# Half of the weights' remainders formed by accumulating DMAs instead of VectorE

## The chip, the cores and the metric

The kernel runs on one core of a Trainium2 chip. The metric is the time of one execution in microseconds on the device; times named here are the median of several runs, and a profile is one further execution, with its own time. The engines are called by their names in the profile: PE (TensorE, the matmuls), DVE (VectorE), ACT (ScalarE), POOL (GpSimd) and SP (SyncE, which here only issues DMAs).

## The reference

The reference is a trunk of two layers on x of 512 tokens by 1024 channels, in float32. Cut to what matters:

```python
for i in range(DEPTH):                       # DEPTH = 2
    xn = rmsnorm(x, norm1_g[i])
    u_pool, q, k, v, g_a, g_b = split(xn @ w_in[i])     # one combined projection
    q = partial_rotary(rmsnorm(q, q_norm_g[i])); k = partial_rotary(rmsnorm(k, k_norm_g[i]))
    o = diff_attention(q, k, v, lam)         # 4 heads, each two softmaxes of 128-wide q and k:
                                             # (p0 - lam * p1) @ v, chunk-causal with chunks of 64
    attn_out = rmsnorm(o, subln_g[i]) * (1.0 - lam_init)
    pool_out = pool_mixer(u_pool, pool_w[i], pool_scale[i])   # windowed means, 4 groups
    merged = sigmoid(g_a) * pool_out + sigmoid(g_b) * attn_out
    x = x + merged @ w_out[i]
    gate, up = split(rmsnorm(x, norm2_g[i]) @ w_ffn_in[i])
    x = x + (silu(gate) * up) @ w_ffn_out[i]
return x
```

## The kernel before

Every product is made in three matmuls of a reduced float format (fp32r): an operand is split into a rounded part, called hi, and its remainder, lo, and a product is hi·hi + hi·lo + lo·hi. So each weight has to be split before PE can use it. The weights come in pieces of 128 x 1024 numbers (512 KB): SP issues a load into a tile `raw` (line 213; seven slots), ACT casts it to `whi`, and DVE subtracts, `wlo = raw - whi` (both line 201, in `split`; six slots each). For some pieces of the feed-forward part there is already another way, lines 225 to 227 in `parts`: ACT casts to `whi`, ACT writes the negated piece, rounded, to `wlo`, and POOL issues a DMA that loads the same piece from memory a second time and adds it to `wlo`. The result is again weight minus rounded weight.

PE's work is written out in program order by the functions below, with a clock of PE columns: `later(delay, what)` queues a step until that clock has gone on by `delay`, and `run_due` starts due steps between matmuls. The order on each engine follows from that and from the scheduler that takes an instruction as its inputs come ready.

In each layer the heads are taken in the order 3, 2, 1, 0 (`ORDER`). A head has three blocks of weights, each of four pieces (`wblock(KD)`, 1024 by 512): the first for q and k, the second for v and one gate (both in `attention`), the third for the pooled branch and the other gate (in `merged`, run behind the next head's attention; the last one behind its own). For each quarter of the tokens (t = 0 to 3) `evicted` makes the squares of q and k (ACT, line 585), a power on POOL (line 335, `r`), and the scaled copy `qn` on DVE (line 589). Outside the first head of layer 0 the transpose goes partly through memory: DVE transposes into `near` (line 305), SP writes it to `away` and reads it back to `near` (lines 306 and 310), and ACT and DVE split it into `qh` and `ql`. Then `scores` multiplies q and k into one of two banks `sc`, ACT takes the exponential (`pr`, line 520), `turn_prob` splits the probabilities into `ah` and `al`, and `weighted` multiplies them with v. The same detour by `near` serves the probabilities and the head's output (`mt`).

The first block of layer 0's head 3 is read by another path (`at_start`) and doesn't come by `wblock`.

Of the kernel before, what the change touches and what calls it, by code (L numbers as in the profile page):

```python
# [23 lines left out]
KD = D // P  # L24
# [26 lines left out]
ORDER = (3, 2, 1, 0)  # L51
# [72 lines left out]
def trunk_kernel(  # L124
# [16 lines left out]
    def mm_ps():  # L141
        return ps.tile([P, 512], F32, name="mm", tag="mm", bufs=6)
# [60 lines left out]
    def split_half(hi, lo, src):  # L203

        half = nc.scalar.activation(hi, src, AF.Copy, scale=0.5)
        return half, nc.vector.scalar_tensor_tensor(lo, src, 0.5, hi.bitcast(F32), op0=ALU.mult, op1=ALU.subtract)

    def loaded():

        i = at[0]  # L210
        at[0] += 1
        raw = sb.tile([P, 2, 512], F32, name="raw", tag="raw", bufs=RAWS)
        transfers.append(nc.sync.dma_start(raw.rearrange("p a b -> p (a b)"), wts[i]))
        return raw, i
# [3 lines left out]
    def parts(raw, piece_no=None):  # L218

        hi = sb.tile([P, 2, 512], F32R, name="whi", tag="whi", bufs=SPLITS)  # L220
        lo = sb.tile([P, 2, 512], F32R, name="wlo", tag="wlo", bufs=SPLITS)
        if piece_no is None:
            made[:] = split(hi, lo, raw)
        else:
            nc.scalar.copy(hi, raw)
            made[0] = nc.scalar.activation(lo, raw, AF.Copy, scale=-1.0)  # L226
            nc.gpsimd.dma_start(lo.rearrange("p a b -> p (a b)"), wts[piece_no], accum_op=ALU.add)  # L227
        return hi, lo

    def rows_of(pair, n=2):  # L230

        hi, lo = (x.rearrange("p a b -> p (a b)").rearrange("p (k c) -> p k c", k=n) for x in pair)
        return [(hi[:, k, :], lo[:, k, :]) for k in range(n)]

    def piece(n=2, by_dma=False):
        raw, i = loaded()
        return rows_of(parts(raw, i if by_dma else None), n)

    def wblock(n):

        return [pair for _ in range(n // 2) for pair in piece()]


    clock = [0]
# [40 lines left out]
    def product(acc, pairs):  # L285

        n = len(pairs)
        for i, ((ah, al), (bh, bl)) in enumerate(pairs):
            run_due()
            nc.tensor.matmul(acc, lhsT=ah, rhs=bh, start=i == 0, stop=False)  # L290
            nc.tensor.matmul(acc, lhsT=ah, rhs=bl, start=False, stop=False)  # L291
            last = nc.tensor.matmul(acc, lhsT=al, rhs=bh, start=False, stop=i == n - 1)  # L292
            clock[0] += 3 * acc.shape[-1]
        return last
# [48 lines left out]
    def need(*keys):  # L343
        run_due(lambda: all(k in ready for k in keys))
# [9 lines left out]
    def pair(name, tag, n):  # L354
        return [sb.tile([P, n, S], F32R, name=name + part, tag=tag, bufs=2) for part in "hl"]
# [117 lines left out]
    for layer in range(L):  # L473
# [8 lines left out]
        def x_all(t0=0, t1=NT):  # L482
            return [(xh[:, k, t0 * P:t1 * P], xl[:, k, t0 * P:t1 * P]) for k in range(KD)]

        def cut(pairs, c0, c1):
            return [(h[:, c0:c1], l[:, c0:c1]) for h, l in pairs]

        def attention(j, before, then):

            if before is not None:  # L490
# [84 lines left out]

            at_start = not layer and j == ORDER[0]
            if not at_start:
                w = wblock(KD)
            held = []

            def evicted(t, acc):
# [33 lines left out]
                need(*((layer, before, "o", t) for t in range(NT)))  # L615
            vh, vl = pair("v", "v", 2)
            tb = [sb.tile([P, 2, VD], F32, name="tb", tag="tb", bufs=2) for _ in range(2)]
            w = wblock(KD)
            if at_start:
                with tc.issue_after(transfers[-1].ins):  # L620
                    for i in range(L):
# [14 lines left out]
        def pool_weights(j):  # L636
            raw = sb.tile([P, 2, VD], F32, name="pwr", tag="raw", bufs=RAWS)
            nc.scalar.dma_start(raw.rearrange("p a b -> p (a b)"), pool_w[layer, j])
            both = sb.tile([P, 2, 2, VD], F32R, name="pw", tag="pw")
            hi, lo = both[:, 0], both[:, 1]  # L640
            split(hi, lo, raw)
            return [(hi[:, a, :], lo[:, a, :]) for a in range(2)]

        def windowed(j, c, acc, uh, ul):

            window = WINDOWS[j]
            up = sb.tile([P, 16 + S], F32, name="up", tag="up", bufs=2)
            nc.vector.memset(up[:, :16], 0.0)
            nc.vector.tensor_mul(up[:, 16:], acc, rms_rows[layer])
            prev, step, n = up, 1, 0  # L650
            while step < window:
                cur = sb.tile([P, 16 + S], F32, name="us", tag="us", bufs=2)
                nc.vector.memset(cur[:, :16], 0.0)
                nc.vector.tensor_add(cur[:, 16:], prev[:, 16:], prev[:, 16 - step:16 + S - step])
                prev, step, n = cur, step * 2, n + 1
            head = sb.tile([P, 16], F32, name="head", tag="head", bufs=2)
            nc.vector.tensor_mul(head, prev[:, 16:32], inv_t[:, j, :])
            nc.vector.scalar_tensor_tensor(
                prev[:, 32:], prev[:, 32:], 1.0 / window, up[:, 32:], op0=ALU.mult, op1=ALU.subtract)
            nc.vector.tensor_sub(prev[:, 16:32], head, up[:, 16:32])  # L660
            split(uh[:, c, :], ul[:, c, :], prev[:, 16:])

        def merged(j, mj, mh, ml):

            w = wblock(KD)
            pw = pool_weights(j)
            uh, ul = pair("u", "u", 2)
            for c in range(2):
                acc = mm_ps()
                product(acc, list(zip(cut(w, c * P, (c + 1) * P), x_all())))  # L670
                windowed(j, c, acc, uh, ul)

            gates = []
            for c in range(2):
                acc = mm_ps()
                product(acc, list(zip(cut(w, VD + c * P, VD + (c + 1) * P), x_all())))
                ta = sb.tile([P, S], F32, name="ta", tag="ta", bufs=2)
                nc.vector.tensor_mul(ta, acc, rms_rows[layer])
                nc.scalar.activation(ta, ta, AF.Tanh, scale=0.5)
                gates.append(ta)  # L680
            need(*((layer, j, "mj", t) for t in range(NT)))
            for c in range(2):
                y = mm_ps()
                product(y, list(zip(cut(pw, c * P, (c + 1) * P), [(uh[:, a, :], ul[:, a, :]) for a in range(2)])))
                ta = gates[c]
                k = KD * layer + 2 * j + c
                nc.vector.scalar_tensor_tensor(ta, ta, 1.0, y, op0=ALU.add, op1=ALU.mult)
                nc.vector.scalar_tensor_tensor(ta, ta, scale[:, k:k + 1], mj[:, c, :], op0=ALU.mult, op1=ALU.add)
                split_half(mh[:, c, :], ml[:, c, :], ta)
# [257 lines left out]
        def mix(i):  # L947
            j = ORDER[i]
            if i == 2:
                need(*((layer, ORDER[3], "s", t) for t in range(NT)))  # L950
                ms[j] = pair("m", "qk", 4)
            else:
                ms[j] = pair("m", "m", 2)
            merged(j, mjs[j], *ms[j])

        for i, j in enumerate(ORDER):
            then = (lambda: project_out(ORDER[i - 2])) if i >= 2 else None
            mjs[j] = attention(j, ORDER[i - 1] if i else None, then)
            if i:
                mix(i - 1)  # L960
# [68 lines left out]
```

## Time and profile before

| | |
|---|---|
| median of 3 runs | 1392.16 us (1390.02 to 1392.28) |
| the profiled execution | 1391.49 us, span of its instructions 1389.7 us |
| mean granted clock of PE | 0.997 |
| PE busy | 1375.8 us, 99% of the span |
| DVE / ACT / POOL busy | 1042.5 / 704.1 / 118.2 us |
| pieces of weights split by DVE | 221 subtractions, 266.7 us |
| pieces with an accumulating DMA | 64, all in the feed-forward parts |
| moved by DMA | 224.52 MB |

In the rows of the profile an operation stands with its line, the engine and "output <- inputs"; x is the count, then come the busy time and the mean of one in nanoseconds, and behind a bar the idle time of the engine just before and what ended it. A row of the timeline has the start, the duration, the engine and the line, and in brackets the idle time before it with its releaser. A row of waits has the waiting operation, the one waited for, the total in microseconds, the count and the longest. A row of stretches has the stretch, the busy time of PE, PE's weight loads, DVE, ACT and POOL with counts, the granted clock, the share of the DMA engines and GB/s. A row of a DMA queue has packets, megabytes and the share of sixteen engines' span.

### The profile page before, as it was taken

What the parts mean: (1) busy time and instruction counts of PE and PEld (TensorE: products, weight loads), DVE (VectorE), ACT (ScalarE), POOL (GpSimd) and SP (SyncE); (2) the same over time, 40 slices, a digit from 0 to 9 for tenths busy, and PEclk for the clock granted to TensorE, in tenths of its full rate; (3) what the DMA queues carried; (4) which work ended last, traced back from release to release, by engine and by line L of the source; (5) the groups of instructions that cost most, each with busy time, mean ns of one, the idle gap of its engine ahead of it and who ended that gap; (6) DMA issues with size and microseconds to landing.
All of it is one profiled execution on the core that took longest, in us unless ns stands there. A gap on an engine that the chain in (4) does not pass through costs nothing.

```text
span 1389.7 us, 18568 instructions
## 1 busy us (share of the span) xinstructions
PE 1375.8 (99%) x6242; PEld 1142.0 (82%) x6242; DVE 1042.5 (75%) x1979; ACT 704.1 (51%) x1321; POOL 118.2 (9%) x139
## 2 busy tenths in 40 slices
PE   9999999999999999999999889999999999999999
PEld 7888888888888888888888778888888888888887
DVE  7778778786869768578667787786868686785782
ACT  7545353454766545564435443444547565554540
POOL 1010100000111001110011100000001010011100
PEclk9999999999999999999999999999999999999999
DMA  8333454444667868686334345534446688687741
GB/s 311 104 124 112 147 162 131 148 136 134 152 181 191 240 177 225 164 208 209 109 121 137 106 135 165 163 122 148 140 129 151 183 199 220 195 219 173 199 129 61
DMA packets 141071, 224.52 MB, mean 162 GB/s; under 512 B 40880, under 2 KB 88496, under 8 KB 140976
## 3 DMA queue, kind: packets, MB, share of 16 engines
q1 hardware_dynamic: 130464, 187.65, 42.1%
q0 software_dynamic: 9216, 33.56, 13.8%
q10 hardware_dynamic: 1296, 2.12, 0.5%
q8 instruction: 49, 0.80, 0.2%
q14 instruction: 46, 0.38, 0.1%
HBM read 194.04 MB, written 29.23 MB: 161 GB/s over the span
## 4 chain that ended last, share of the span: by engine, by line
PE 93%; DVE 3%; issue 1%; DMA 1%; POOL 1%; ACT 0%; SPq 0%; DVEq 0%; POOLq 0%; ACTq 0%
PE mm L272 14%; PE mm L273 14%; PE mm L271 14%; PE mm L292 13%; PE mm L290 13%; PE mm L291 13%; PE sc L271 3%; PE sc L273 3%; PE sc L272 3%; PE sc L291 1%; PE sc L292 1%; PE sc L290 1%; DVE qn L589 1%; POOL r L335 1%; DVE wlo L201 1%
## 5 line engine op out<-in xcount | busy, mean ns | idle before, releaser
L201 DVE TENSOR_TENSOR wlo<-raw,whi 128x1024 fp32r<-128x1024 f32 (+1 forms) x221 | 266.7, 1211 | 62.9 <-ACT whi L201 62.3
L201 ACT CAST whi<-raw 128x1024 fp32r<-128x1024 f32 (+1 forms) x221 | 229.9, 1047 | 165.0 <-PE mm L273 60.3
L290 PE MATMUL mm<-whi,xh 128*128 128x512 f32 x480 | 189.0, 394 | 0.0
L291 PE MATMUL mm<-wlo,xh 128*128 128x512 f32 x480 | 187.5, 391 | 0.0
L292 PE MATMUL mm<-whi,xl 128*128 128x512 f32 x480 | 187.3, 390 | 0.0
L273 PE MATMUL mm<-fh,wlo 128*128 128x512 f32 (+1 forms) x356 | 137.8, 387 | 0.0
L272 PE MATMUL mm<-fl,whi 128*128 128x512 f32 (+1 forms) x356 | 137.8, 387 | 0.0
L271 PE MATMUL mm<-fh,whi 128*128 128x512 f32 (+1 forms) x356 | 137.8, 387 | 0.0
L692 DVE TENSOR_TENSOR res<-mm,res 128x512 f32<-128x512 f32 (+1 forms) x145 | 98.1, 680 | 43.1 <-PE mm L273 41.8
L292 PEld LDWEIGHTS mm<-whi,xl 128*128 128x128 f32 x480 | 90.3, 188 | 19.2
L290 PEld LDWEIGHTS mm<-whi,xh 128*128 128x128 f32 x480 | 90.4, 188 | 17.4
L291 PEld LDWEIGHTS mm<-wlo,xh 128*128 128x128 f32 x480 | 90.5, 188 | 17.2
L227 POOL DMA_DIRECT2D wlo<-in_wts x64 | 56.1, 877 | 536.8 <-ACT wlo L226 364.1
L335 POOL TENSOR_TENSOR r<-r,mhalf 128x1 f32<-128x1 f32 (+1 forms) x64 | 56.4, 882 | 528.8 <-DVE r L334 509.0
L291 PE MATMUL mm<-xl,whi 128*128 128x512 f32 x256 | 100.4, 392 | 0.0
L290 PE MATMUL mm<-xh,whi 128*128 128x512 f32 x256 | 100.3, 392 | 0.0
L292 PE MATMUL mm<-xh,wlo 128*128 128x512 f32 x256 | 100.0, 391 | 0.0
L273 PE MATMUL mm<-whi,xl 128*128 128x512 f32 x224 | 87.2, 389 | 0.0
L271 PE MATMUL mm<-whi,xh 128*128 128x512 f32 x224 | 87.2, 389 | 0.0
L272 PE MATMUL mm<-wlo,xh 128*128 128x512 f32 x224 | 87.2, 389 | 0.0
L226 ACT ACTIVATE wlo<-raw 128x1024 fp32r<-128x1024 f32 x64 | 67.7, 1057 | 29.0 <-PE mm L272 27.3
L271 PEld LDWEIGHTS mm<-fh,whi 128*128 128x128 f32 x356 | 66.9, 188 | 13.6
(217 smaller groups left out, 2939.4 us busy)
## 6 DMA issues: line engine op xcount, KB each, us to landing
raw<-in_wts SPq DMA_DIRECT2D x243, 512.0 KB, 3.9
wlo<-in_wts POOLq DMA_DIRECT2D x64, 512.0 KB, 6.1
away<-near SPq DMA_DIRECT2D x72, 256.0 KB, 2.4
near<-away SPq DMA_DIRECT2D x288, 64.0 KB, 2.5
away<-near SPq DMA_DIRECT2D x28, 128.0 KB, 1.7
near<-away SPq DMA_DIRECT2D x112, 32.0 KB, 2.5
pwr<-in_pool_w ACTq DMA_DIRECT2D x8, 256.0 KB, 2.7
away<-pr SPq DMA_DIRECT2D x7, 256.0 KB, 2.0
```

Of the source, the lines that this page charges most:

```text
L201: return nc.scalar.copy(hi, src), nc.vector.tensor_sub(lo, src, hi.bitcast(F32))
L226: made[0] = nc.scalar.activation(lo, raw, AF.Copy, scale=-1.0)
L227: nc.gpsimd.dma_start(lo.rearrange("p a b -> p (a b)"), wts[piece_no], accum_op=ALU.add)
L271: nc.tensor.matmul(acc, lhsT=ah, rhs=bh, start=start, stop=False, **check)
L272: nc.tensor.matmul(acc, lhsT=ah, rhs=bl, start=False, stop=False, **check)
L273: last = nc.tensor.matmul(acc, lhsT=al, rhs=bh, start=False, stop=stop, **check)
L290: nc.tensor.matmul(acc, lhsT=ah, rhs=bh, start=i == 0, stop=False)
L291: nc.tensor.matmul(acc, lhsT=ah, rhs=bl, start=False, stop=False)
L292: last = nc.tensor.matmul(acc, lhsT=al, rhs=bh, start=False, stop=i == n - 1)
L335: nc.gpsimd.tensor_tensor(r, r, mhalf[:, :width], op=ALU.pow)
L589: nc.vector.scalar_tensor_tensor(qn[:, h, :], acc[:, h * QK:(h + 1) * QK], r[:, h:h + 1], g, op0=ALU.mult, op1=ALU.mult)
L692: return nc.vector.tensor_add(res[d][:, cs], acc, res[d][:, cs])
```

## The change

In every block of every head, except the blocks of head 3 in layer 0, the first two of the four pieces now get their remainder in the way of lines 225 to 227: a cast and a negated copy on ACT, and an accumulating DMA issued by POOL. The other two pieces stay with DVE. That is 9 blocks in layer 0 and 12 in layer 1, so 42 pieces. Lines behind the new function carry numbers three higher than before.

```diff
-    def wblock(n):
-
-        return [pair for _ in range(n // 2) for pair in piece()]
+    def wblock(n, by_dma=0):
+
+        return [pair for i in range(n // 2) for pair in piece(2, i < by_dma)]
...
+        def by_dma(j):
+            return 2 if layer or j != ORDER[0] else 0
+
         def attention(j, before, then):
...
             if not at_start:
-                w = wblock(KD)
+                w = wblock(KD, by_dma(j))
...
-            w = wblock(KD)
+            w = wblock(KD, by_dma(j))
             if at_start:
...
         def merged(j, mj, mh, ml):
 
-            w = wblock(KD)
+            w = wblock(KD, by_dma(j))
             pw = pool_weights(j)
```

The scheduler puts the instructions in another order in places. On DVE, in the first head of layer 1 (at 717 to 723 us of the profile before; `wlo_7050` and `wlo_7056` are remainders of the block for v, `near_6714` the transposed q and k of a quarter), the row before was:

```order
L201 TENSOR_TENSOR wlo_6799<-raw_6796,whi_6798 128x1024
L362 TENSOR_TENSOR m12_6709<-qn_6695,tab_68 128x128
L366 TENSOR_TENSOR m12_6709<-qn_6695,tab_68 128x4x16 x2
L201 TENSOR_TENSOR wlo_7050<-raw_7047,whi_7049 128x1024
L367 TENSOR_TENSOR qn_6695<-m12_6709 128x4x32
L201 TENSOR_TENSOR ql_6527<-near_6635,qh_6526 128x4x128
L201 TENSOR_TENSOR wlo_7056<-raw_7053,whi_7055 128x1024
L305 STREAM_TRANSPOSE near_6714<-qn_6695 128x4x4x32
```

and now, at the same place on DVE (other numbers for the same tiles), it is:

```order
L201 TENSOR_TENSOR wlo_6821<-raw_6818,whi_6820 128x1024
L362 TENSOR_TENSOR m12_6729<-qn_6715,tab_68 128x128
L366 TENSOR_TENSOR m12_6729<-qn_6715,tab_68 128x4x16 x2
L201 TENSOR_TENSOR ql_6545<-near_6655,qh_6544 128x4x128
L367 TENSOR_TENSOR qn_6715<-m12_6729 128x4x32
L305 STREAM_TRANSPOSE near_6734<-qn_6715 128x4x4x32
```

Two subtractions are gone, and ql stands one place further ahead.

On PE, at 57 to 61 us, in layer 0, the scores of the first head's last quarter (`sc_633` and `sc_640`) stood in the middle of the second head's projection (`mm_679`):

```order
L290 MATMUL mm_679<-whi_663,xh_113 128x512
L291 MATMUL mm_679<-wlo_664,xh_113 128x512
L292 MATMUL mm_679<-whi_663,xl_114 128x512
L290 MATMUL mm_679<-whi_663,xh_113 128x512
L291 MATMUL mm_679<-wlo_664,xh_113 128x512
L290 MATMUL sc_633<-qh_230 128x512
L291 MATMUL sc_633<-ql_231,qh_230 128x512
```

and now stand on PE three matmuls earlier in it (`mm_681` is that projection's tile in the changed program):

```order
L290 MATMUL mm_681<-whi_664,xh_113 128x512
L291 MATMUL mm_681<-wlo_665,xh_113 128x512
L290 MATMUL sc_633<-qh_230 128x512
L291 MATMUL sc_633<-ql_231,qh_230 128x512
L292 MATMUL sc_633<-qh_230,ql_231 128x512
L290 MATMUL sc_640<-qh_230 128x512
L291 MATMUL sc_640<-ql_231,qh_230 128x512
L292 MATMUL sc_640<-qh_230,ql_231 128x512
L292 MATMUL mm_681<-whi_664,xl_114 128x512
```

Three matmuls of the projection moved behind the six of the scores. The same happens at 744 us, in layer 1, with two matmuls; the rest of PE's order is as before.

On POOL the issues now stand between the powers of line 335. Its order in layer 0, from 30 us on (`r_357` is the power of the first head's last quarter), was:

```order
L335 TENSOR_TENSOR r_326<-r_326,mhalf_69 128x4
L335 TENSOR_TENSOR r_357<-r_357,mhalf_69 128x4
L335 TENSOR_TENSOR r_705<-r_705,mhalf_69 128x1
L335 TENSOR_TENSOR r_722<-r_722,mhalf_69 128x4
L335 TENSOR_TENSOR r_790<-r_790,mhalf_69 128x1
```

and is now, on POOL:

```order
L335 TENSOR_TENSOR r_326<-r_326,mhalf_69 128x4
L227 DMA wlo_658<-in_wts 128x1024
L335 TENSOR_TENSOR r_357<-r_357,mhalf_69 128x4
L227 DMA wlo_665<-in_wts 128x1024
L227 DMA wlo_1002<-in_wts 128x1024
L227 DMA wlo_1009<-in_wts 128x1024
L335 TENSOR_TENSOR r_707<-r_707,mhalf_69 128x1
```

One issue came ahead of the fourth power, and three came between it and the fifth. Each waits for the negated copy on ACT that precedes it.

## The prediction

> **What bounds the kernel now.** I read the page first, for the engines' shares, the chain that ended last and the price of each operation.
>
> ```profile
> PE 1375.8 (99%) x6242; PEld 1142.0 (82%) x6242; DVE 1042.5 (75%) x1979; ACT 704.1 (51%) x1321; POOL 118.2 (9%) x139
> ...
> q0 software_dynamic: 9216, 33.56, 13.8%
> ...
> PE 93%; DVE 3%; issue 1%; DMA 1%; POOL 1%; ACT 0%; SPq 0%; DVEq 0%; POOLq 0%; ACTq 0%
> ...
> L201 DVE TENSOR_TENSOR wlo<-raw,whi 128x1024 fp32r<-128x1024 f32 (+1 forms) x221 | 266.7, 1211 | 62.9 <-ACT whi L201 62.3
> ...
> L227 POOL DMA_DIRECT2D wlo<-in_wts x64 | 56.1, 877 | 536.8 <-ACT wlo L226 364.1
> ...
> L226 ACT ACTIVATE wlo<-raw 128x1024 fp32r<-128x1024 f32 x64 | 67.7, 1057 | 29.0 <-PE mm L272 27.3
> ...
> wlo<-in_wts POOLq DMA_DIRECT2D x64, 512.0 KB, 6.1
> ```
>
> PE is busy 99% of the span and makes 93% of the chain. VectorE, which the change relieves, has 3% of the chain. So relief pays only where PE stands still. Busy time in stretches shows where that is, and PE's waits show on whom:
>
> ```profile
> 100.00:700.00 600.00, 599.97 (x2707) 499.34 (x2706) 460.26 (x808) 312.60 (x537) 46.57 (x53) 1.00 0.59 165
> 700.00:750.00 50.00, 49.14 (x231) 40.92 (x230) 35.16 (x99) 23.03 (x68) 5.84 (x6) 1.00 0.41 133
> 750.00:800.00 50.00, 46.16 (x215) 38.20 (x214) 37.25 (x103) 23.89 (x71) 6.45 (x8) 0.97 0.39 116
> 800.00:850.00 50.00, 46.40 (x209) 38.01 (x208) 39.05 (x99) 17.75 (x52) 5.01 (x6) 0.97 0.50 157
> ```
>
> ```profile
> PE mm L290 <- ACT ah L201: 6.4, 2, 3.2
> ...
> PE sc L290 <- ACT pr L520: 0.9, 1, 0.9
> PE sc L291 <- DVE ql L201: 0.5, 1, 0.5
> PE mm L292 <- DVE up L648: 0.4, 1, 0.4
> ```
>
> From 100 to 700 us, which holds most of layer 0's changed heads, PE idles 0.03 us in 600. The idle time to be had is at the start of layer 1: 0.86, 3.84 and 3.60 us. The waits end on ACT's casts of the probabilities (ah, twice, 3.2 us the longest), on an exponential (pr), and on DVE's ql and up. None ends on a wlo, the tile the change makes in another way.
>
> **The change, part by part.** It removes 42 subtractions on DVE: 42 x 1.211 = 51 us. It adds 42 negated copies on ACT (42 x 1.057 = 44 us) and 42 DMA issues on POOL (42 x 0.877 = 37 us), each of 512 KB that lands after 6.1 us. The 64 such DMAs of before take 13.8% of sixteen engines' span, 191.8 us, or 3.0 us each; 42 more take 126 us. All these engines have room on average (ACT 51%, POOL 9%), and none of the totals is on PE's path. The first two pieces of a block fill the two spare slots of the six-slot ring, so their remainders are made about a block ahead of use; the 0.9 + 6.1 us of issue and landing is covered by that lead, and if it were gone PE would wait up to those 7 us per block. The raw tile is now freed by ACT's negated copy instead of DVE's subtraction; the loads queued on SP behind it have seven slots of lead. So the sum is made stall by stall.
>
> *Stall A, 3.24 us at 769.6.* PE waits for ah:
>
> ```profile
> 769.60 0.39 PE L290 MATMUL mm<-vh,ah 128*128 128x256 f32 x1 [3.24 <-ACT ah L201]
> ```
>
> ```profile
> 765.73 0.39 ACT L555 ACTIVATE mt<-mm 128x256 f32<-128x256 f32 x1 [2.05 <-DVE near L305]
> ...
> 766.10 2.92 ACT L201 CAST whi<-raw 128x1024 fp32r<-128x1024 f32 x3
> 768.93 0.62 ACT L201 CAST ah<-pr 128x512 fp32r<-128x512 f32 x1
> ```
>
> ```profile
> 765.26 0.43 DVE L305 STREAM_TRANSPOSE near<-mt 128x256 f32<-128x256 f32 x1
> ...
> 766.42 1.22 DVE L201 TENSOR_TENSOR wlo<-raw,whi 128x1024 fp32r<-128x1024 f32 x1
> ```
>
> Three whi casts of 2.92 us stand ahead of ah on ACT, and they start when DVE's near (765.26) lets the square at 765.73 go. DVE's work behind that is the eviction of a projection that PE triggers at 753; the timeline has no subtraction on DVE there until 766.42, after the trigger. In the changed order the three casts still stand ahead of ah, and both negated copies behind it. Change 0; between 0 and +1.06, one negated copy, if ACT came to it sooner.
>
> *Stall B, 3.15 and 0.40 us at 817 to 821.* Its chain runs through DVE's work on the pooled branch:
>
> ```profile
> 820.61 0.39 PE L290 MATMUL mm<-vh,ah 128*128 128x256 f32 x1 [3.15 <-ACT ah L201]
> ```
>
> ```profile
> 803.69 0.69 DVE L649 TENSOR_TENSOR up<-mm,hg 128x512 f32<-128x512 f32 x1 [1.86 <-PE mm L292]
> ```
>
> DVE idles 1.86 us before 803.69 for PE, so what it saves on the two subtractions ahead of that becomes longer idling, and no subtraction follows until 826. Change 0.
>
> *Stall C, 0.86 us at 732.4*, is the one with removed work on its chain:
>
> ```profile
> 719.25 1.22 DVE L201 TENSOR_TENSOR wlo<-raw,whi 128x1024 fp32r<-128x1024 f32 x1
> ...
> 720.58 0.69 DVE L201 TENSOR_TENSOR ql<-near,qh 128x512 fp32r<-128x512 f32 x1
> 721.18 1.22 DVE L201 TENSOR_TENSOR wlo<-raw,whi 128x1024 fp32r<-128x1024 f32 x1
> 722.32 0.71 DVE L305 STREAM_TRANSPOSE near<-qn 128x512 f32<-128x512 f32 x1
> ```
>
> ```profile
> 729.96 0.61 ACT L201 CAST qh<-near 128x512 fp32r<-128x512 f32 x1
> 730.59 1.28 ACT L520 ACT_TABLE_LOAD   x1
> 731.88 0.37 ACT L520 ACTIVATE pr<-sc,mx 128x128 f32<-128x128 f32 x1
> ```
>
> ```profile
> 732.39 0.39 PE L290 MATMUL sc<-qh 128*128 128x256 f32 x1 [0.86 <-ACT pr L520]
> ```
>
> ```profile
> 720.00:730.00 10.00, 10.00 (x52) 8.45 (x51) 7.76 (x22) 3.27 (x14) 1.01 (x1) 1.00 0.71 233
> ```
>
> Both subtractions go, so near starts not at 722.32 but where the rest of DVE's row allows, at about 720.2: 2.1 us earlier. But near then goes out to memory and comes back by DMA before qh (end of near 723.03 to qh 729.96, 6.9 us), and the two remainders of this block now travel at that very time: their negated copies end at about 718 and 720.5, and with the landing of 6.1 us they are under way to 727. They ask 2 x 3.0 = 6.0 us of all DMA engines in a window that is 0.71 full and has 2.9 of 10 us free. The round trip grows by between 0 and 6.0 us; I take 2.1, a little under the overflow of 3.1, since part of the first DMA is over before near goes out. Then gain and loss cancel: stall C changes by 0, between -0.86 and +3.9 (6.0 less 2.1).
>
> *Two places where PE's own order changes.* The scores of the last block of tokens move three matmuls ahead (layer 0) and two (layer 1):
>
> ```profile
> 58.98 0.50 PE L290 MATMUL sc<-qh 128*128 128x512 f32 x1
> ...
> 744.07 0.39 PE L290 MATMUL sc<-qh 128*128 128x512 f32 x1
> ```
>
> ```profile
> 58.26 0.58 ACT L520 ACTIVATE pr<-sc,mx 128x384 f32<-128x384 f32 x1 [0.24 <-DVE mx L519]
> ...
> 742.84 0.58 ACT L520 ACTIVATE pr<-sc,mx 128x384 f32<-128x384 f32 x1
> ```
>
> The scores need the bank that these exponentials free. Matmuls in a row start 0.227 us apart, so at 59 us they are wanted 0.68 us earlier; before, the first exponential ended at 58.84, 0.14 ahead of need, and a subtraction less on DVE brings it forward by about 0.4. 0.68 - 0.14 - 0.4 = +0.14, taken as +0.2 (0 to +0.7). At 744 they are wanted 0.45 us earlier, and ACT, with a negated copy more in front, exponentiates some 0.4 later; before, the first of them ended at 743.42, 0.65 ahead of need. 0.45 + 0.4 - 0.65 = +0.2 (0 to +0.9).
>
> The stall on ql (0.5) has a chain without subtractions: 0. Sum: +0.4. The profiled execution took 1391.49 us, 0.67 under the median of the three runs (1392.16) and inside their spread; the median of all four is 1391.8. Forecast: 1391.8 + 0.4 = 1392.2 us, no measurable change (0.2%, or 2.8 us, is about what a measurement of this kernel can tell from none).
>
> [...] The 64 issues on POOL take 877 ns in the mean, beside a DVE that is busy 75%, and their longest is 1.06 us, so that row prices an issue. [...]
>
> **The rivals.**
>
> *Layer 1's stalls go with VectorE's relief* (faster). If DVE's queue, and not its triggers, set A or B, one would vanish: 3.2 us and the clock's loss behind it:
>
> ```profile
> 770.00:780.00 10.00, 9.94 (x45) 8.28 (x45) 6.23 (x13) 3.01 (x16) 0.00 (x0) 0.83 0.40 123
> ```
>
> A granted clock of 0.83 over 10 us is 1.7 us lost after a stall of over 3 us; after the 0.86 one none is. So one stall is worth 4.9 us (1387.3), both with C and the small ones 11.5 (1380.7). [...] Against it: no removed subtraction lies on either chain. [...]
>
> *The added transfers lengthen near's round trip* (slower). Place: stall C. At the full 6.0 us the stall is 0.86 + 3.9 = 4.8 us and costs the 1.7 us of clock too: +5.6, 1397.8. It decides from a growth of 4.9 us on (2.1 gained and 2.8 to be seen); below 1.2 the stall is gone. For it: 0.71 of the window is taken. Against it: away and near are small beside the weights.
>
> *The issues hold up POOL's powers* (slower). POOL works in order, and an eviction waits for its power:
>
> ```profile
> 34.04 1.01 POOL L335 TENSOR_TENSOR r<-r,mhalf 128x4 f32<-128x4 f32 x1 [2.12 <-DVE r L334]
> ```
>
> ```profile
> 31.39 0.61 ACT L201 CAST qh<-mm 128x512 fp32r<-128x512 f32 x1
> ```
>
> Ahead of this power now stands an issue that waits for a negated copy: 32.0 + 1.06 + 0.88 = 33.9, just before 34.04. It decides where the copy comes later; each such case delays an eviction by up to 1 us, and only where banks are short does PE feel it. Three or four would give 1395 to 1396.
>
> That the change does nothing can be left out: the orders show 42 issues more on POOL.
>
> **How the numbers follow.** The forecast, with its small terms at their bounds, has 0.74: 1390.5 to 1394.5. One of A and B gone (1387.3) 0.08, both 0.02; the round trip 0.10; POOL's powers 0.05; other 0.01. By these cases faster 0.11 (the other case counted in), same 0.74, slower 0.15. The range of eight in ten, 1387.0 to 1396.5, reaches to one stall gone and to all but the full growth of the round trip.
>
> **What would show it.** In the changed profile: DVE about 51 us less busy, ACT 44 more, POOL 37 more, q0 up to about 23%; PE still 99%; the two waits on ah of about 3.2 us and the clock's dips behind them; near about 2 us earlier at 720 and the accumulating DMAs landing around it; PE waits of some 0.2 us ahead of the scores at 59 and 744. I am wrong if a wait on ah is gone or shorter than 3 us, if PE waits for a wlo, or if the wait for the exponential at 732 exceeds 3 us.

## The result, and the profile after

The changed kernel took 1439.51 us in the median of 4 runs (1433.54 to 1442.66), against 1391.82 for the kernel before in the same session: a ratio of 1.034, with a 95% interval of 1.030 to 1.038. It is 48 us slower, where no measurable change was forecast. Its profiled execution has a span of 1440.7 us, 51.0 more than before.

The page of the changed kernel, the same rows as before (engines, queue, chain, the three operations, the landing):

```profile
PE 1397.1 (97%) x6242; PEld 1153.5 (80%) x6242; DVE 1003.0 (70%) x1937; ACT 740.0 (51%) x1363; POOL 152.2 (11%) x181
...
q0 software_dynamic: 15264, 55.58, 22.0%
...
PE 73%; DMA 7%; DVE 5%; ACT 3%; SPq 2%; issue 1%; POOL 1%; DVEq 0%; ACTq 0%; POOLq 0%
...
L201 DVE TENSOR_TENSOR wlo<-raw,whi 128x1024 fp32r<-128x1024 f32 (+1 forms) x179 | 215.9, 1211 | 62.7 <-ACT whi L201 62.3
...
L227 POOL DMA_DIRECT2D wlo<-in_wts x106 | 94.1, 888 | 791.8 <-ACT wlo L226 491.6
...
L226 ACT ACTIVATE wlo<-raw 128x1024 fp32r<-128x1024 f32 x106 | 112.2, 1061 | 29.1 <-PE mm L272 26.3
...
wlo<-in_wts POOLq DMA_DIRECT2D x106, 512.0 KB, 7.0
```

The work moved as counted: 51 us of subtractions less on DVE, 44.5 us of negated copies more on ACT, 38 us of issues more on POOL. (The busy times moved by 39.5, 35.9 and 34.0. On DVE and ACT instructions overlap in the traces, as the subtraction of 717.64 to 718.86 us and its follower at 718.77 before, and the busy time counts such stretches once: the durations added up moved by 50.0 and 45.5. On POOL the powers took 3.5 us less.) The chain tells that this is not what matters: DMA, 1% of it before, now has 7%, and PE fell from 93% to 73%. PE idles 43.6 us in the span (1440.7 - 1397.1) where it idled 13.9: 29.7 us more. The other 21.3 of the 51.0 are in PE's busy time, which rose from 1375.8 to 1397.1 with the same 6242 matmuls. About 17 of them are the clock: the trace has PE busy for 40 us at a granted clock of 0.5, in spells of 3.41 or 6.83 us at the stalls, where before had 7. What makes up the other 4 is not shown. The stretches and PE's waits show where:

```profile
150.00:200.00 50.00, 45.45 (x198) 37.28 (x197) 30.11 (x86) 20.88 (x60) 7.93 (x9) 0.97 0.64 170
200.00:250.00 50.00, 46.95 (x215) 39.23 (x214) 35.98 (x80) 23.24 (x46) 4.00 (x6) 0.97 0.59 164
...
300.00:350.00 50.00, 45.09 (x197) 36.92 (x196) 36.03 (x78) 22.31 (x44) 3.98 (x6) 0.93 0.55 157
...
400.00:720.00 320.00, 320.00 (x1417) 265.07 (x1416) 231.85 (x304) 173.91 (x222) 26.35 (x30) 1.00 0.74 196
720.00:770.00 50.00, 45.91 (x204) 37.93 (x203) 27.18 (x81) 24.82 (x67) 7.75 (x8) 0.93 0.51 135
```

```profile
PE sc L290 <- ACT pr L523: 13.8, 7, 4.1
PE mm L290 <- ACT ah L201: 11.9, 7, 3.1
PE mm L292 <- DVE al L201: 11.4, 6, 2.6
```

The stalls are in the heads of both layers, where layer 0 had next to none (0.3 us at 70); its feed-forward part (400 to 720) still has none. PE waits for the exponentials and for both parts of the probabilities, never for a remainder by DMA. Stall C of the prediction shows the way. The chain of the changed kernel there, in order of time (start, duration, what):

```profile
748.03 8.35 DMA away<-near
...
757.77 2.23 DMA near<-away
...
760.10 0.62 ACT qh L201
...
760.73 1.28 ACT L523
...
762.03 0.47 ACT pr L523 x2
...
762.54 0.58 PE sc L290
```

The trip out to memory alone takes 8.35 us. From the end of near's transpose to qh it is 12.2 us (747.90 to 760.10) where it was 6.9. The DMA issues between 100 and 360 us, first of before, then of the changed kernel, show the same on two of the trips of the probabilities (KB each, median us to landing, here of two or three):

```profile
away<-pr SPq DMA_DIRECT2D x3, 192.0 KB, 3.1
...
away<-pr SPq DMA_DIRECT2D x2, 64.0 KB, 2.5
```

```profile
wlo<-in_wts POOLq DMA_DIRECT2D x14, 512.0 KB, 8.6
near<-away SPq DMA_DIRECT2D x40, 64.0 KB, 2.1
...
away<-pr SPq DMA_DIRECT2D x3, 192.0 KB, 8.1
...
away<-pr SPq DMA_DIRECT2D x3, 64.0 KB, 6.7
```

A DMA of 64 KB that landed in 2.5 us took 6.7 with the accumulating DMAs under way. Not every trip is longer: in this stretch the median of near's returns of 64 KB is 2.1 us in both kernels. Of the 28 trips of the probabilities out to memory in the heads, 10 took over 5 us, where before none did.

### The profile page after: what moved, and what is told of

It reads as the page before. It is cut to its first block, busy times and chain, and to the rows that moved or that the text cites. A ratio compares the mean times of both kernels' runs of the same rounds, so it can differ in the third digit from the quotient of the medians.

```text
span 1440.7 us, 18697 instructions
## 1 busy us (share of the span) xinstructions
PE 1397.1 (97%) x6242; PEld 1153.5 (80%) x6242; DVE 1003.0 (70%) x1937; ACT 740.0 (51%) x1363; POOL 152.2 (11%) x181
## 4 chain that ended last, share of the span: by engine, by line
PE 73%; DMA 7%; DVE 5%; ACT 3%; SPq 2%; issue 1%; POOL 1%; DVEq 0%; ACTq 0%; POOLq 0%
PE mm L272 14%; PE mm L273 14%; PE mm L271 14%; PE mm L292 8%; PE mm L290 7%; PE mm L291 7%; PE sc L271 3%; PE sc L273 3%; PE sc L272 3%; DMA away<-pr 2%; DMA away<-near 2%; SPq L310 1%; DMA near<-away 1%; ACT whi L201 1%; POOL r L335 1%
## 5 line engine op out<-in xcount | busy, mean ns | idle before, releaser
L201 DVE TENSOR_TENSOR wlo<-raw,whi 128x1024 fp32r<-128x1024 f32 (+1 forms) x179 | 215.9, 1211 | 62.7 <-ACT whi L201 62.3
L201 ACT CAST whi<-raw 128x1024 fp32r<-128x1024 f32 (+1 forms) x179 | 185.8, 1046 | 122.0 <-PE mm L273 60.0
L227 POOL DMA_DIRECT2D wlo<-in_wts x106 | 94.1, 888 | 791.8 <-ACT wlo L226 491.6
L225 ACT CAST whi<-raw 128x1024 fp32r<-128x1024 f32 x106 | 110.6, 1045 | 46.4 <-PE mm L291 25.3
L226 ACT ACTIVATE wlo<-raw 128x1024 fp32r<-128x1024 f32 x106 | 112.2, 1061 | 29.1 <-PE mm L272 26.3
L335 POOL TENSOR_TENSOR r<-r,mhalf 128x1 f32<-128x1 f32 (+1 forms) x64 | 52.9, 828 | 370.4 <-DVE r L334 350.3
```

The lines of the kernel that those rows point to most:

```text
L201: return nc.scalar.copy(hi, src), nc.vector.tensor_sub(lo, src, hi.bitcast(F32))
L335: nc.gpsimd.tensor_tensor(r, r, mhalf[:, :width], op=ALU.pow)
```

## The experiments

The theories: (A) the accumulating DMAs slow the detour through memory; (B) the negated copies delay ACT; (C) the order that the scheduler chose for the changed program is worse. Times are medians; each ratio is to runs of the kernel before on the same chip (1391.9 to 1392.2 us).

**e_no_dma: everything but the DMAs.**

```diff
         made[0] = nc.scalar.activation(lo, raw, AF.Copy, scale=-1.0)
-        nc.gpsimd.dma_start(lo..., wts[piece_no], accum_op=ALU.add)
+        if dma:                              # False for the pieces of the heads
+            nc.gpsimd.dma_start(lo..., wts[piece_no], accum_op=ALU.add)
```

> The changed kernel with the 42 accumulating DMAs of the heads left out: casts and negated copies stay on ACT, POOL issues nothing for them, and the remainder of these pieces stays the negated copy alone, so the output is another one. PE's and ACT's orders are those of the changed kernel. If the transfers cause the loss by lengthening the detour of near and pr through memory (theory A), the stalls of the heads go and the time is 1386 to 1393 us. If the negated copies in front of ACT's casts and exponentials cause it (B), or the order that the scheduler chose for the changed program (C), it stays at 1425 to 1442 us.

1391.28 us, ratio 0.9999 (0.9989 to 1.0008). The whole loss is gone, with casts, negated copies and orders of PE and ACT as in the changed kernel. B and C fall. The waits of PE in this kernel (lines one further on):

```profile
PE mm L291 <- ACT ah L201: 6.4, 2, 3.3
...
PE sc L292 <- DVE ql L201: 0.5, 1, 0.5
PE mm L293 <- DVE up L652: 0.4, 1, 0.4
```

The two long waits on ah are those of before; the wait on the exponential at 732 (stall C, 0.9) is missing. So relieving DVE of 51 us, with ACT's copies in exchange, is worth nothing that can be measured even where the DMAs cost nothing.

**e_plain: plain copies for the accumulating DMAs.**

```diff
-            nc.gpsimd.dma_start(lo..., wts[piece_no], accum_op=ALU.add)
+            nc.gpsimd.dma_start(lo..., wts[piece_no].bitcast(F32R))     # heads only
```

> The changed kernel with the 42 DMAs of the heads as plain copies of the same 512 KB, without adding, so that the remainder is the weight itself and the output another one. All orders are those of the changed kernel. If it is the adding that makes the DMA engines slow (A1), the DMAs land in about 4 us as the raw loads do, and the time falls to 1395 to 1415 us. If it is the bytes, or that POOL issues them (A2), it stays at 1425 to 1442. B and C: 1425 to 1442.

1399.59 us, ratio 1.0059 (1.0044 to 1.0074): 8 us lost instead of 48 with the same bytes, issues and orders. The queue's row:

```profile
q0 software_dynamic: 15264, 55.58, 18.6%
```

Less the 191.8 us of the feed-forward part's 64, that is 18.6% of 1395.9 - 191.8 = 68 us for 42 plain DMAs, 1.6 us of sixteen engines each. For the changed kernel it is 22.0% of 1440.7 - 191.8 = 125 us, 3.0 each. So an accumulating DMA took nearly twice the engines' time here. POOL's issues stand in the same places in this run, though shorter (755 ns in the mean, against 888), so the prediction's rival that they hold up POOL's powers has room for some of these 8 us and hardly more.

**e_zero: before's work, with accumulating DMAs of zeros.**

```diff
-        return [pair for i in range(n // 2) for pair in piece(2, i < by_dma)]
...                                              # zeros: 512 KB in memory, written once at the start
+        def one(i):
+            raw, _ = loaded()
+            hi, lo = parts(raw)                  # DVE subtracts, as before
+            if i < by_dma:
+                nc.gpsimd.dma_start(lo..., zeros, accum_op=ALU.add)
+            return rows_of((hi, lo))
```

> The kernel before, with DVE's subtractions kept and no negated copy on ACT, and behind the subtraction of the same 42 pieces an accumulating DMA that adds 512 KB of zeros from memory to the remainder. Traffic and POOL's issues as in the changed kernel, ACT's work as before. A: 1420 to 1445 us. B: 1388 to 1396. C: between, since the scheduler orders this program anew.

1441.88 us, ratio 1.0351 (1.0331 to 1.0371). The DMAs alone, with DVE and ACT as before, bring the loss: 50 us. (This program was ordered anew in places, on ACT and SP too.)

**e_one: one piece of four.**

```diff
-            return 2 if layer or j != ORDER[0] else 0
+            return 1 if layer or j != ORDER[0] else 0
```

> The changed kernel with one piece of four by DMA instead of two: 21 accumulating DMAs. A: each detour meets one DMA and not two, and the leads written into the order cover part of that: 1398 to 1415 us. B: half the copies, 1410 to 1420. C: 1420 to 1442.

1403.70 us, ratio 1.0092 (1.0071 to 1.0113): 12 us for 21 DMAs, 48 for 42. The loss is not in proportion. A reading of that, argued and not shown: a lead covers a growth up to its own length, and only what exceeds it is a stall. The traces fit it. In the heads there are 84 detours; counted from SP's issue to the landing of the last return, 2 of them took over 10 us before, 17 here and 27 in the changed kernel; over 12 us it was none, 4 and 10. How long each lead is was not measured.

**f_lead and f_lead_before: longer leads.**

```diff
-QK_AWAY, SCORE_AWAY, PROB_AWAY, AV_AWAY, MERGE_AWAY = 28000, 26000, 32000, 18000, 24000
+QK_AWAY, SCORE_AWAY, PROB_AWAY, AV_AWAY, MERGE_AWAY = 38000, 26000, 42000, 22000, 28000
```

> The changed kernel with longer leads written into the order: the steps that use what comes back from memory are queued later, q and k by 10000 columns of PE's clock (4.4 us at 0.227 us for 512), the probabilities by 10000, the product with v and the head's output by 4000 (1.8 us). If the accumulating DMAs lengthen the detour by 4 to 6 us and the leads of the order no longer cover it (theory A), the stalls of the heads shrink to a third or less: 1392 to 1408 us. If the DMAs slow something else (loads of weights, the remainders themselves), the time stays at 1430 to 1445.

> The same longer leads in the kernel before, as a control for what they do without the DMAs. Before, only four places wait, all at the start of layer 1: A expects 1380 to 1396 us, gaining where the lead of the probabilities was short there, losing where the tiles in flight (two of the probabilities, three of q and k) hold a step back.

1431.57 us (ratio 1.0285, 1.0269 to 1.0300) with the DMAs, and 1399.08 (1.0050, 1.0035 to 1.0065) without. Both expectations missed. The DMAs still cost 32 us under these leads instead of 48, so the leads take off a third and not two thirds, and they cost 7 by themselves. PE's idle time hardly fell (1429.0 - 1386.5 = 42.5 us, against 43.6); 12.8 of it is now a single wait on ah. The time lies in the range given to the rival that the DMAs slow loads or remainders. PE's waits speak against that rival: 18.0 us on the exponentials, 16.5 on ah, 2.3 on al, and 0.2 on a remainder (DVE's). The chain of f_lead at one remaining stall shows why a lead does not cover it:

```profile
1005.79 1.74 DMA pr<-away
...
1007.69 0.30 ACT ah L201
...
1009.29 1.98 ACT whi L201 x2
1011.27 0.96 ACT wlo L226
1012.23 0.93 ACT whi L225
...
1013.54 0.93 ACT whi L225
...
1014.74 0.68 ACT pr L523 x2
...
1015.46 0.79 PE sc L290
```

A late return holds ah at the head of ACT's queue. Five weights' operations behind it, 4.8 us, follow in their order, and only then comes the exponential that PE's bank waits for. In ACT's fixed order this late trip delays work that has nothing to do with it.

**g_av and g_prob: before, with one lead changed.** They try the two long waits of before, which the rival of the faster side was about.

```diff
-... PROB_AWAY, AV_AWAY, ... = ... 32000, 18000, ...
+... PROB_AWAY, AV_AWAY, ... = ... 32000, 26000, ...     # g_av
+... PROB_AWAY, AV_AWAY, ... = ... 28000, 18000, ...     # g_prob
```

> The kernel before with one lead alone made longer: the product of the probabilities with v is queued 8000 columns (3.5 us) later. The two longest waits of before (3.2 us each, on the cast ah at the start of layer 1) should go, with the half clock behind each (1.7 us): 1381 to 1386 us. If the cast is late because of PE's own order, it moves along and the time stays at 1390 to 1394.

> The kernel before without any added DMA, with one lead shorter: the step that casts the returned probabilities (ah, al) is queued 4000 columns (1.8 us) earlier, so that ACT's order has ah ahead of some of the three casts of weights that stood before it at the start of layer 1. If the two waits of 3.2 us come from that order alone, one or both shrink: 1381 to 1388 us. If the probabilities come back no earlier and ACT now waits for them at the head of its queue, 1390 to 1400.

g_av: 1391.61 us, ratio 0.9996 (0.9987 to 1.0006). A wait on ah of 2.9 us and one on al of 3.3 us stand in its profile: the waits moved and did not go. g_prob: 1395.46 us, ratio 1.0025 (1.0014 to 1.0035), slower. No version faster than before was found.

**e_double and e_double2: two plain DMAs for each accumulating one.** Open after e_plain was whether the adding counts as such, or the engines' time.

```diff
             nc.gpsimd.dma_start(lo..., wts[piece_no].bitcast(F32R))
+            nc.gpsimd.dma_start(scratch, wts[piece_no])           # e_double
+            nc.gpsimd.dma_start(scratch, hi...)                   # e_double2
```

> As e_plain (plain copies in place of the 42 accumulating DMAs, so the output is another one), and behind each copy POOL issues a second plain DMA of the same 512 KB to a scratch place in memory, whose result nothing uses. Two plain DMAs keep the sixteen engines busy for about 2 x 1.6 = 3.2 us by e_plain's share of q0, one accumulating DMA for 3.0. If it is the engines' time that the detour waits for, the loss comes back: 1425 to 1445 us. If it is the adding as such, little more than e_plain: 1398 to 1410.

> As e_plain (plain copies for the 42 accumulating DMAs, the output is another one), and for each of the 42 pieces POOL issues one more plain DMA of 512 KB, from the cast tile whi to a scratch place in memory that nothing reads. It waits for the same cast on ACT, so it travels with the first, which e_double's second DMAs did not: they waited for nothing and ran at the start. By e_plain the engines need about 1.6 us for a plain DMA and 3.0 for an accumulating one; two plain ones make 3.2. If the detour waits for the engines' time, the loss of the changed kernel comes back: 1425 to 1445 us, near's and pr's trips 7 to 9 us. If it is the adding as such: 1398 to 1412 us.

e_double took 1428.67 us (1.0261, 1.0243 to 1.0279), but tells nothing: its second DMAs waited for no cast, and 22 of 42 were issued in the first 60 us, where PE then waited 11.8 us at once. e_double2 took 1444.88 us (1.0378, 1.0353 to 1.0404). Its queue, and the trips of the probabilities between 100 and 360 us:

```profile
q0 software_dynamic: 21312, 77.60, 22.7%
```

```profile
again<-whi POOLq DMA_DIRECT2D x14, 512.0 KB, 5.7
wlo<-in_wts POOLq DMA_DIRECT2D x14, 512.0 KB, 8.1
...
away<-pr SPq DMA_DIRECT2D x3, 192.0 KB, 8.0
...
away<-pr SPq DMA_DIRECT2D x3, 64.0 KB, 6.9
```

22.7% of 1442.4 - 191.8 = 136 us for 84 plain DMAs, again 1.6 each, so 3.2 for a pair against 3.0 for an accumulating one. The trips are 8.0 and 6.9 us against 8.1 and 6.7, and the loss is 53 us against 48. So the loss goes with the time of the engines, and not with the adding as such.

The sizes fit a simple sum only in part. Two pieces of a block travel together and ask 2 x 3.0 us of all engines. Added to the 3.1 us of the 192 KB trip that is 9.1, and the trip took 8.1. With plain copies it is 3.1 + 2 x 1.6 = 6.3, and the trip took 5.3:

```profile
away<-pr SPq DMA_DIRECT2D x3, 192.0 KB, 5.3
```

With one accumulating DMA a block (e_one) the sum is 6.1, but the trips took nearly as long as beside two:

```profile
away<-pr SPq DMA_DIRECT2D x3, 192.0 KB, 7.7
...
away<-pr SPq DMA_DIRECT2D x2, 64.0 KB, 6.1
```

Why one such DMA lengthens a trip by more than its 3.0 us stays open.

DMAs that POOL issues lengthen trips that SP issues: with two accumulating ones a block, those of 192 KB took 8.1 us where they took 3.1. Why such a DMA kept the engines busy for 3.0 us and a plain one for 1.6, no run shows.

**e_qk, e_vg and e_ug: the DMAs in one block of each head.** `by_dma(j)` stays at one of the three calls of `wblock` and is taken from the other two.

```diff
-            w = wblock(KD, by_dma(j))     # at two of the three blocks
+            w = wblock(KD)
```

> The changed kernel with the DMAs in the first block of each head only (q and k): 14 in place of 42. In the changed trace these are in flight with the return of near for q and k, ahead of the waits on pr. If each block's DMAs cost by the detours they meet, the three blocks add up to the 48 us lost: here 10 to 22, 1402 to 1414 us. If the loss comes only from all together (DMA engines full over the head), here 1392 to 1398.

> The DMAs in the second block of each head only (v and gate): 14. In the changed trace they meet near's return for the third and fourth quarter and the first trip of pr: 8 to 20 us lost, 1400 to 1412 us; from all together only: 1392 to 1398.

> The DMAs in the third block only (pooled branch and gate): 14. In the changed trace they meet the trips of pr and of the head's output, ahead of the waits on ah and al: 10 to 20 us lost, 1402 to 1412 us; from all together only: 1392 to 1398.

| | us | ratio (interval) | lost |
|---|---|---|---|
| e_qk | 1403.77 | 1.0077 (1.0061 to 1.0094) | 11.7 |
| e_vg | 1405.12 | 1.0090 (1.0075 to 1.0105) | 13.0 |
| e_ug | 1410.58 | 1.0134 (1.0119 to 1.0150) | 18.5 |

All three are in the expected ranges, and the losses add up to 43 of 48 us. No block is a harmless place, and the loss doesn't need all three together. That each pair of DMAs costs by the trips that it meets is the reading that fits.

## Why the prediction was wrong

*Right:* the count of the work (42 pieces, the prices per operation); no removed subtraction on the chains of A and B, which the run without the DMAs kept at 6.4 us; and the gain at stall C: in that run near follows 3.6 us behind the start of the scaled copies `qn` and not 5.7, 1.3 us of this reach the exponential, and C is gone. POOL's issues hardly slowed (888 ns in the mean after 877, the longest 1.20 us after 1.06), and PE never waited for a remainder made by DMA. The two terms of +0.2 at 59 and 744 us did not show: without the DMAs no such wait is listed.

*A size that was wrong:* "The round trip grows by between 0 and 6.0 us; I take 2.1". It grew by 5.3 us at that place (12.2 against 6.9) in spite of the earlier start, and stall C went from 0.86 to 4.1 us, a change of +3.2 under an upper bound of +3.9. The argument for the low value, that there were 2.9 us free in ten, took free time of a window for free time of the trip: the two DMAs (issued at 745.13 and 747.55) and the trip (748.03) want the engines in the same few microseconds.

*The step that failed:* "So the sum is made stall by stall." It took the places where before had stalls and left out those that had none. The price of a longer trip was worked out at one of them, while 42 DMAs go out in 21 blocks and the detours of seven heads lie beside them. "From 100 to 700 us ... PE idles 0.03 us in 600" says that the leads cover the trips at their old length of about 2.5 us; it says nothing of how much more they cover. With 4 to 5 us more on a trip that meets the DMAs (6.7 for 2.5, 8.1 for 3.1, stall C's 12.2 for 6.9) they often did not, in layer 0 as in layer 1: 42 DMAs cost 48 us.

The rival "the added transfers lengthen near's round trip" named the mechanism, with 0.10 and 1397.8 us. Its error is the same: it was priced at stall C alone, and its own argument against, that near is small beside the weights, holds the other way round: with two DMAs of 512 KB under way, near's trip out at 748 took 8.35 us, and the probabilities' trips of 64 KB took 6.7 for 2.5.

The other rival, of the faster side, had 1.7 us of clock lost behind a stall of over 3 us. Shorter waits had it too: in the changed kernel two of 0.95 and 2.09 us, at 236 and 239, were followed by 3.41 us at a clock of 0.5, as before the waits of 3.24 and 3.15 us were. How short a wait must be to spare the clock, no run shows.

A row of the trace before could have hinted at the price. The DMA issues of before between 100 and 360 us, with two accumulating DMAs, and between 380 and 690, with 26:

```profile
near<-away SPq DMA_DIRECT2D x36, 64.0 KB, 2.1
...
wlo<-in_wts POOLq DMA_DIRECT2D x2, 512.0 KB, 7.2
```

```profile
wlo<-in_wts POOLq DMA_DIRECT2D x26, 512.0 KB, 6.2
...
near<-away SPq DMA_DIRECT2D x88, 64.0 KB, 3.5
```

The same transfer of 64 KB had a median of 2.1 us where such DMAs were rare and of 3.5 where they were common, 8.3 the longest. The queue of SP's own DMAs took about the same share in both stretches (41.7 and 44.9%), POOL's 2.1 and 25.4%. It is a hint and no proof. The prediction read the landing of the added DMAs and not what they do to others.

Open stays what leads would cover the trips: the one longer set tried took off a third of the loss, and at the start of layer 1 it has a stall of 12.8 us.

## What to carry to other kernels

A transfer that is itself hidden need not be free (here 42 of 512 KB cost 48 us): ask which small transfers on the path go out while it is under way, measure how long such a trip gets beside it, and hold that against every lead in the order, those with no stall above all. The engines' time of what is in flight is a first estimate of the growth, and can be too low (here 3.0 us against 4.6 beside one accumulating DMA). No stall in a profile means a lead of unknown length, not an unlimited one. Where the relieved engine doesn't set the end, even the free version of the relief (here the run without the DMAs, 1391.28 us for 1391.94) can be worth nothing, and that can be tried first.

## What was not expected of the hardware

An accumulating DMA of 512 KB kept the sixteen engines busy for 3.0 us where a plain one took 1.6, and 42 of them cost about as much as 84 plain ones (48 and 53 us lost). Beside two of them a transfer of 64 KB went from 2.5 to 6.7 us, and beside one to 6.1. And the loss grows faster than the number: 21 cost 12 us, 42 cost 48, of which about 17 us are PE's lower clock at the stalls and not the stalls themselves.
